# Feed-forward weight sums in half units with two buffers, row norms as columns with a diagonal, and three subtractions on another engine

## The chip, the cores and the metric

The kernel runs on one core of a Trainium2 chip. A core has a matrix engine (TensorE, in the profile PE for its matmuls and PEld for its weight loads), VectorE (DVE), ScalarE (ACT), GpSimd (POOL) and SyncE (SP). Here every data transfer is issued by SP, on one queue. Each engine takes its instructions strictly in order and waits on semaphores for the others. The metric is device microseconds of one execution.

## The reference

One encoder block over 1040 tokens (16 learned ones and 1024) of width 1024, all in float32. A root-mean-square norm feeds one wide input projection. Its parts go to a four-head bidirectional retention in chunks of 128 tokens, and to a bidirectional state-space scan (SSD); both results are projected, gated and merged, and added to the input. A second norm feeds a feed-forward network (FFN), and a last norm ends the block:

```python
y_ret = head_group_norm(y_ret).reshape(b, l, RET_V) * ret_gn_w
y_ret = (jax.nn.silu(g_ret) * y_ret) @ w_ret_out
...
merged = jax.nn.sigmoid(gate_ret) * y_ret + jax.nn.sigmoid(gate_ssd) * y_ssd
h = h + merged @ w_out
f = dw_conv_centred(rms_norm(h, norm_ffn_w) @ w_ffn_up, w_ffn_conv, b_ffn_conv)
fg, fu = _split(f, (D_FF, D_FF))
h = h + (jax.nn.silu(fg) * fu) @ w_ffn_down
...
h = rms_norm(h, final_norm_w)
return h[:, N_META:]
```

where `rms_norm(x, w)` is x / sqrt(mean(x*x) + 1e-6) * w over the 1024 features of a token.

## The kernel before

Features lie on the 128 partitions (eight tiles for 1024) and tokens along the free axis. Float32 products are made of three matmuls on a high and a low half of each operand (`mm3`, lines 143 to 145); a weight tile is loaded as `wraw` (L132), and ACT and DVE split it into `whi` (L135) and `wlo` (L136).

The program runs through these stages, with times of the profiled execution: the first norm and the first projections (0 to 52 us); the retention of heads 0 to 3, each merged step by step with the dense projections of the next head (52 to 520); SSD (520 to 1410); the output projections (1410 to 1810); the second norm and the FFN's first product (1770 to 2210); its second product and the last norm (2210 to the end).

A scheduler places the instructions of each engine: the code only gives lists of steps, and `merge` and `spread` interleave them. Three places matter here.

**The sums.** The FFN's first product multiplies 2 x 2 blocks in a scheme with fewer products, which needs sums of weight blocks. They depend on weights alone, and are made early: `sum_steps` (L488 to 513) gives a load, an add and a store step for each of 22 units, and L566 spreads six units each over the dense steps beside heads 0 to 2, and four beside head 3. A unit loads two tiles of 128 x 1024 (L494 and L495, 512 KB each, single buffers named `ws`), makes four POOL operations of 128 x 512 in place (L501 to 504), and stores both tiles to a scratch tensor in DRAM (L508). The next unit's loads reuse the tiles, so each must wait for a store.

The retention uses POOL too: rotary products `sw` (L338), scaled queries `qd` (L429), and for each chunk two tiny operations on `bs` (L448, L449: variance plus epsilon, to the power of minus one half), which DVE needs to write the normalised `ry` (L451), which PE transposes to `ptr` (L459).

**The norm before the FFN** (`norm2_steps`, L1041 to 1073). Squares are summed over the eight feature tiles into `acc`. `scale` (L1053) multiplies a 128 x 128 matrix of ones with 128 x n sums, so that each partition holds the sums of all n tokens, takes the square root on ACT (L1058) and the reciprocal on DVE (L1059), both 128 x n. `norm` (L1065) multiplies the eight feature tiles of `hb`. Then differences of operands are formed: t1 (L1068), t3 (L1070) and t4 (L1072) on POOL, t2 (L1071) on DVE; each operand is split into a high half (ACT, L1050) and a low half (DVE, L1051). This is done for two rounds of tokens.

**The last norm** (`fin` in `last_down`, L1318 on). For four blocks of 256 tokens: a matmul with ones (L1320), square root (L1321), reciprocal (L1322), and products with eight feature tiles on DVE (L1329) and POOL (L1327), and the stores. The `fin` of a block is placed after the third feature tile of the next block, the last one at the end.

Of the kernel before, what the change touches and what calls it, by code (L numbers as in the profile page):

```python
# [8 lines left out]
F32 = mybir.dt.float32  # L9
# [7 lines left out]
P = 128  # L17
D = 1024
# [77 lines left out]
def hybrid_kernel(ctx, tc, t):  # L96
# [214 lines left out]
    rb = []  # L311
# [175 lines left out]

    def sum_steps(js):  # L488
        steps = []
        tl = {}  # L490

        def load(j):
            a, b = [rb[0].tile([P, 1024], F32, name=f"ws{i}", tag=f"ws{i}", bufs=1) for i in range(2)]
            nc.sync.dma_start(out=a, in_=t["w_up"][j])  # L494
            nc.sync.dma_start(out=b, in_=t["w_up"][NF + j])  # L495
            tl[j] = a, b

        def add(j):
            a, b = tl[j]
            a11, a12, a21, a22 = a[:, :512], a[:, 512:], b[:, :512], b[:, 512:]  # L500
            nc.gpsimd.tensor_tensor(a22, a21, a22, op=ALU.add)  # L501
            nc.gpsimd.tensor_sub(a21, a11, a21)  # L502
            nc.gpsimd.tensor_sub(a11, a22, a11)  # L503
            nc.gpsimd.tensor_sub(a12, a12, a11)

        def store(j):
            for i, x in enumerate(tl.pop(j)):
                nc.sync.dma_start(out=ws_d[j][:, i, :], in_=x)  # L508

        for j in js:  # L510
            for f in (load, add, store):
                steps.append((0.0, lambda f=f, j=j: f(j)))
        return steps

    def spread(a, b):
# [47 lines left out]
    for h in range(HR):  # L563
        steps = ret_steps(h, str_[h])
        dense = ret_dense(h + 1, str_[h + 1]) if h + 1 < HR else z_steps(0)[:-3]
        dense = spread(dense, sum_steps(((0, 6), (6, 12), (12, 18), (18, 22))[h][0] + i for i in range((6, 6, 6, 4)[h])))  # L566
        merge(steps[:-2], dense, left, 3)
        left = steps[-2:]
# [470 lines left out]
    wo = wo_es.enter_context(tc.tile_pool(name="wo", bufs=2, side="right"))  # L1039

    def norm2_steps(r, acc):  # L1041
        t0 = RB[r][0][0]
# [10 lines left out]
        def scale(q):  # L1053
            b0, bn = RB[r][q]
            ps = pm.tile([P, 512], F32, name="psn", tag="psm")
            x = acc[:, b0 - t0:b0 - t0 + bn]
            nc.tensor.matmul(ps[:, :bn], ones, x, start=True, stop=True)
            nc.scalar.activation(x, ps[:, :bn], AF.Sqrt, bias=eps, scale=1.0 / D)  # L1058
            nc.vector.reciprocal(x, x)  # L1059

        def norm(d0, q):
            b0, bn = RB[r][q]
            for d in range(d0, d0 + 4):
# [3 lines left out]
        steps = [lambda: scale(0), lambda: norm(0, 0), lambda: scale(1), lambda: norm(0, 1),  # L1067
                 lambda: put("b11", u[0][0]), lambda: nc.gpsimd.tensor_sub(t1, u[0][1], u[0][0]),  # L1068
                 lambda: norm(4, 0), lambda: put("b21", u[1][0]), lambda: norm(4, 1), lambda: put("t1", t1),
                 lambda: put("b22", u[1][1]), lambda: nc.gpsimd.tensor_sub(t3, u[1][1], u[0][1]),  # L1070
                 lambda: nc.vector.tensor_sub(t2, u[1][1], t1), lambda: put("t2", t2),  # L1071
                 lambda: nc.gpsimd.tensor_sub(t4, u[1][0], t2), lambda: put("t3", t3), lambda: put("t4", t4)]  # L1072
        return steps
# [240 lines left out]
    def last_down():  # L1314
# [3 lines left out]
        def fin(t0, n, acc, last):  # L1318
            ps = pm.tile([P, 512], F32, name="psn", tag="psm")
            nc.tensor.matmul(ps[:, :n], ones, acc[:, :n], start=True, stop=True)  # L1320
            nc.scalar.activation(acc[:, :n], ps[:, :n], AF.Sqrt, bias=eps, scale=1.0 / D)  # L1321
            nc.vector.reciprocal(acc[:, :n], acc[:, :n])  # L1322
            for d in range(KT):
# [137 lines left out]
```

## Time and profile before

| | |
|---|---|
| three timed runs | 2543.72 to 2549.94 us, median 2547.14 us |
| the profiled execution | 2538.35 us |
| its span, first to last instruction | 2536.6 us |
| mean granted TensorE clock | 0.973 |
| PE busy | 2390.3 us, 94% of the span |
| DVE, ACT, POOL busy | 1324.4, 841.2, 786.5 us |
| the stretch that holds the sums | 52.6 us (first load) to 334.3 us (last store) |

The profiled execution was 8.79 us faster than the median of the timed runs, and 1.75 us of its time lie outside the span. A clock of 1.00 in a row is 2.4 GHz; the other level is 1.2 GHz, so that a mean of 0.93 is a mixture of both.

### The profile page before, as it was taken

To read this page: it belongs to the slowest core of one execution; us is meant where nothing else is said; L and a number is where in the kernel's file an instruction comes from. 1 tells how busy PE (TensorE), PEld (TensorE's weight loads), DVE (VectorE), ACT (ScalarE), POOL (GpSimd) and SP (SyncE) were. 2 spreads that over 40 slices of the span, in tenths; PEclk is the share of its full clock that TensorE was granted. 3 is DMA by queue.
4 is the path that set the end of the run, shared out by engine and by line. 5 is a ranking of instruction groups with operands and counts; after the bars stand their busy time and mean duration, and the time that the engine had idled before them with its cause. 6 is when DMAs were issued, how large, how long until landed. Compare 5 with 4: busy or idle time off the path is not lost.

```text
span 2536.6 us, 39605 instructions
## 1 busy us (share of the span) xinstructions
PE 2390.3 (94%) x15836; PEld 2233.6 (88%) x15836; DVE 1324.4 (52%) x1911; ACT 841.2 (33%) x1437; POOL 786.5 (31%) x851
## 2 busy tenths in 40 slices
PE   7888899989999989998999899999899999999997
PEld 7877799988879779888988799999899999998887
DVE  6223234354663563365356434343997777775437
ACT  4211121143353244254323412123454444442204
POOL 2555532113651561373256112222321111110003
PEclk9998999999989999998999999999999999999999
DMA  4666521212571373267146655236444444355111
GB/s 155 215 193 214 197 90 55 61 48 94 158 173 46 129 183 83 70 183 141 52 140 180 173 158 150 88 98 176 132 145 125 118 117 118 116 170 187 67 50 68
DMA packets 162025, 324.43 MB, mean 128 GB/s; under 512 B 20721, under 2 KB 78577, under 8 KB 157745
## 3 DMA queue, kind: packets, MB, share of 16 engines
q1 hardware_dynamic: 161840, 321.90, 42.7%
q8 instruction: 124, 2.03, 0.4%
q14 instruction: 61, 0.49, 0.1%
HBM read 241.57 MB, written 80.27 MB: 127 GB/s over the span
## 4 chain that ended last, share of the span: by engine, by line
PE 65%; DMA 12%; POOL 9%; DVE 7%; issue 3%; ACT 3%; SPq 0%; POOLq 0%; DVEq 0%; ACTq 0%
PE psu L1168 17%; PE psd L143 11%; PE psd L145 11%; PE psd L144 11%; DMA ws<-in_w_up 4%; PE psw L144 3%; PE psw L143 3%; PE psw L145 3%; DMA br<-row 2%; DMA ws<-ws 2%; POOL t L868 1%; POOL ws L503 1%; PE pss L797 1%; POOL ws L502 1%; PE psb L818 1%
## 5 line engine op out<-in xcount | busy, mean ns | idle before, releaser
L143 PE MATMUL psd<-uh,whi 128*128 128x342 f32 (+3 forms) x1376 | 467.5, 340 | 10.6 <-ACT gs L291 6.3
L144 PE MATMUL psd<-ul,whi 128*128 128x342 f32 (+3 forms) x1376 | 447.7, 325 | 0.0
L145 PE MATMUL psd<-uh,wlo 128*128 128x342 f32 (+3 forms) x1376 | 446.6, 325 | 0.0
L135 ACT CAST whi<-wraw 128x1024 fp32r<-128x1024 f32 (+1 forms) x144 | 149.3, 1038 | 515.7 <-PE psd L144 300.1
L136 DVE TENSOR_TENSOR wlo<-wraw,whi 128x1024 fp32r<-128x1024 f32 (+1 forms) x144 | 191.2, 1330 | 214.4 <-ACT whi L135 214.2
L143 PEld LDWEIGHTS psd<-uh,whi 128*128 128x128 f32 (+1 forms) x1376 | 265.0, 193 | 20.7 <-issue 7.9
L144 PEld LDWEIGHTS psd<-ul,whi 128*128 128x128 f32 (+1 forms) x1376 | 264.2, 192 | 7.2 <-issue 6.8
L145 PEld LDWEIGHTS psd<-uh,wlo 128*128 128x128 f32 (+1 forms) x1376 | 263.9, 192 | 0.1
L143 PE MATMUL psd<-whi,uh 128*128 128x256 f32 x768 | 233.5, 304 | 0.4 <-ACT uh L219 0.4
L145 PE MATMUL psd<-whi,ul 128*128 128x256 f32 x768 | 217.1, 283 | 3.2 <-POOL ul L221 2.7
L144 PE MATMUL psd<-wlo,uh 128*128 128x256 f32 x768 | 217.4, 283 | 0.0
L143 PEld LDWEIGHTS psd<-whi,uh 128*128 128x128 f32 x768 | 146.8, 191 | 10.9 <-issue 8.5
L144 PEld LDWEIGHTS psd<-wlo,uh 128*128 128x128 f32 x768 | 147.1, 192 | 5.8 <-issue 5.3
L144 PE MATMUL psw<-ahl,whi 128*128 128x512 f32 (+1 forms) x400 | 148.4, 371 | 1.6 <-DVE ahl L1287 1.6
L145 PEld LDWEIGHTS psd<-whi,ul 128*128 128x128 f32 x768 | 146.4, 191 | 3.9 <-POOL ul L221 3.1
L143 PE MATMUL psw<-ahl,whi 128*128 128x512 f32 (+1 forms) x400 | 147.0, 370 | 0.0
L145 PE MATMUL psw<-ahl,wlo 128*128 128x512 f32 (+1 forms) x400 | 145.8, 366 | 0.0
L143 PE MATMUL psd<-krh,whi 128*128 128x342 f32 x384 | 123.2, 321 | 3.3 <-ACT krh L974 3.3
L144 PE MATMUL psd<-krl,whi 128*128 128x342 f32 x384 | 123.3, 322 | 0.3 <-DVE krl L975 0.3
L145 PE MATMUL psd<-krh,wlo 128*128 128x342 f32 x384 | 123.1, 321 | 0.0
L1227 DVE SCALAR_TENSOR_TENSOR hb<-hb,vec 128x1024 f32<-128x1024 f32 x88 | 111.2, 1280 | 0.4 <-ACT hb L1223 0.2
L1312 DVE TENSOR_TENSOR hb<-psw,hb 128x512 f32<-128x512 f32 x80 | 55.0, 690 | 100.0 <-PE psw L145 99.9
(307 smaller groups left out, 6183.9 us busy)
## 6 DMA issues: line engine op xcount, KB each, us to landing
br<-row SPq DMA_DIRECT2D x32, 1024.0 KB
ws<-in_w_up SPq DMA_DIRECT2D x44, 512.0 KB
ws<-ws SPq DMA_DIRECT2D x44, 512.0 KB
gt<-gate SPq DMA_DIRECT2D x72, 171.0 KB
wraw<-in_w_xbc SPq DMA_DIRECT2D x24, 512.0 KB
wraw<-ws SPq DMA_DIRECT2D x47, 256.0 KB
hb<-ws SPq DMA_DIRECT2D x45, 256.0 KB
act<-hb SPq DMA_DIRECT2D x22, 512.0 KB
```

The costliest lines, as they stand in the source:

```text
L135: nc.scalar.copy(hi[:, :n], raw[:, :n])
L136: nc.vector.tensor_sub(lo[:, :n], raw[:, :n], hi[:, :n].bitcast(F32))
L143: nc.tensor.matmul(ps, ah, bh, start=(i == 0), stop=False)
L144: nc.tensor.matmul(ps, ah, bl, start=False, stop=False)
L145: nc.tensor.matmul(ps, al, bh, start=False, stop=(i == n - 1))
L502: nc.gpsimd.tensor_sub(a21, a11, a21)
L503: nc.gpsimd.tensor_sub(a11, a22, a11)
L797: nc.tensor.matmul(ps, bk(c), st[("xw", d, c)][:n], start=True, stop=True)
L818: nc.tensor.matmul(ps[:n, :], tk("ct", c - 1), st[("pb", c)], start=True, stop=True)
L1168: nc.tensor.matmul(ps[:, :n], a[:, c], b[:, k, :], start=start and k + i == 0, stop=k == 3 and i == 2, skip_group_check=True)
L1227: nc.vector.scalar_tensor_tensor(o[half], f[half][:, 1 + tap:1 + tap + SEQ], V("fconv_w", 3 * fi + tap), o[half], op0=ALU.mult, op1=ALU.add)
L1312: nc.vector.tensor_tensor(hs, ps, hs, op=ALU.add)
```

## The change

The sums are cut into 44 half units. Half unit u takes 256 of the 512 columns of each half row of unit u // 2, so each of its tiles is [128, 2, 256] (256 KB, in pieces of 1 KB) in place of [128, 1024] (512 KB, rows of 4 KB). Each tile name has two buffers. The steps begin with the loads of half units 0 and 1, and after each store comes the load of the half unit two further. Heads 0 to 2 are given twelve half units each and head 3 eight. The POOL operations are 128 x 256.

`row_rms` takes the place of the ones matmul, square root and reciprocal of both norms. With the sums of squares as the stationary operand and one column of ones as the moving one, it gets the token sums as columns (tokens on partitions, two or three columns), takes root and reciprocal of these [w, k] values, scales the identity by them on ACT to a diagonal [w, w] for each column, multiplies ones by the diagonal on PE, which spreads each token's factor over all partitions, and copies the result from PSUM to `acc` on ACT.

The differences t1, t3 and t4 are formed on DVE.

```diff
--- before.py
+++ after.py
@@ -485,32 +485,42 @@
         return steps
 
 
-    def sum_steps(js):
+    def sum_steps(us):
+
+
         steps = []
-        tl = {}
-
-        def load(j):
-            a, b = [rb[0].tile([P, 1024], F32, name=f"ws{i}", tag=f"ws{i}", bufs=1) for i in range(2)]
-            nc.sync.dma_start(out=a, in_=t["w_up"][j])
-            nc.sync.dma_start(out=b, in_=t["w_up"][NF + j])
-            tl[j] = a, b
-
-        def add(j):
-            a, b = tl[j]
-            a11, a12, a21, a22 = a[:, :512], a[:, 512:], b[:, :512], b[:, 512:]
+
+        def part(src, s_):
+            return src.rearrange("p (h s c) -> p s h c", h=2, s=2)[:, s_]
+
+        def load(u):
+            j, s_ = u // 2, u % 2
+            a, b = [rb[0].tile([P, 2, 256], F32, name=f"ws{i}", tag=f"ws{i}", bufs=2) for i in range(2)]
+            nc.sync.dma_start(out=a, in_=part(t["w_up"][j], s_))
+            nc.sync.dma_start(out=b, in_=part(t["w_up"][NF + j], s_))
+            wsum[u] = a, b
+
+        def add(u):
+            a, b = wsum[u]
+            a11, a12, a21, a22 = a[:, 0, :], a[:, 1, :], b[:, 0, :], b[:, 1, :]
             nc.gpsimd.tensor_tensor(a22, a21, a22, op=ALU.add)
             nc.gpsimd.tensor_sub(a21, a11, a21)
             nc.gpsimd.tensor_sub(a11, a22, a11)
             nc.gpsimd.tensor_sub(a12, a12, a11)
 
-        def store(j):
-            for i, x in enumerate(tl.pop(j)):
-                nc.sync.dma_start(out=ws_d[j][:, i, :], in_=x)
-
-        for j in js:
-            for f in (load, add, store):
-                steps.append((0.0, lambda f=f, j=j: f(j)))
+        def store(u):
+            for i, x in enumerate(wsum.pop(u)):
+                nc.sync.dma_start(out=part(ws_d[u // 2][:, i, :], u % 2), in_=x)
+
+        for u in us:
+            if u == 0:
+                steps += [(0.0, lambda: load(0)), (0.0, lambda: load(1))]
+            steps += [(0.0, lambda u=u: add(u)), (0.0, lambda u=u: store(u))]
+            if u + 2 < 2 * NF:
+                steps.append((0.0, lambda u=u: load(u + 2)))
         return steps
+
+    wsum = {}
 
     def spread(a, b):
 
@@ -563,7 +573,7 @@
     for h in range(HR):
         steps = ret_steps(h, str_[h])
         dense = ret_dense(h + 1, str_[h + 1]) if h + 1 < HR else z_steps(0)[:-3]
-        dense = spread(dense, sum_steps(((0, 6), (6, 12), (12, 18), (18, 22))[h][0] + i for i in range((6, 6, 6, 4)[h])))
+        dense = spread(dense, sum_steps(range(12 * h, min(12 * h + 12, 2 * NF))))
         merge(steps[:-2], dense, left, 3)
         left = steps[-2:]
     merge([], z_steps(0)[-3:], left, 2)
@@ -1038,6 +1048,25 @@
     wo_es = ExitStack()
     wo = wo_es.enter_context(tc.tile_pool(name="wo", bufs=2, side="right"))
 
+    def row_rms(x, n):
+
+
+        k = (n + P - 1) // P
+        w = n // k
+        ps = pm.tile([P, 512], F32, name="psn", tag="psm")
+        q = sg.tile([P, 342], F32, name="rms", tag="gt", bufs=2)
+        for i in range(k):
+            nc.tensor.matmul(ps[:w, i:i + 1], x[:, i * w:(i + 1) * w], ones[:, 0:1], start=True, stop=True)
+        r = q[:w, n:n + k]
+        nc.scalar.activation(r, ps[:w, :k], AF.Sqrt, bias=eps[:w], scale=1.0 / D)
+        nc.vector.reciprocal(r, r)
+        ps = pm.tile([P, 512], F32, name="psn", tag="psm")
+        for i in range(k):
+            c = slice(i * w, (i + 1) * w)
+            nc.scalar.activation(q[:w, c], ident[:w, :w], AF.Copy, scale=r[:, i:i + 1])
+            nc.tensor.matmul(ps[:, c], ones[:w], q[:w, c], start=True, stop=True)
+        nc.scalar.copy(x, ps[:, :n])
+
     def norm2_steps(r, acc):
         t0 = RB[r][0][0]
         m = RB[r][0][1] + RB[r][1][1]
@@ -1052,11 +1081,8 @@
 
         def scale(q):
             b0, bn = RB[r][q]
-            ps = pm.tile([P, 512], F32, name="psn", tag="psm")
             x = acc[:, b0 - t0:b0 - t0 + bn]
-            nc.tensor.matmul(ps[:, :bn], ones, x, start=True, stop=True)
-            nc.scalar.activation(x, ps[:, :bn], AF.Sqrt, bias=eps, scale=1.0 / D)
-            nc.vector.reciprocal(x, x)
+            row_rms(x, bn)
 
         def norm(d0, q):
             b0, bn = RB[r][q]
@@ -1065,11 +1091,11 @@
                 nc.vector.scalar_tensor_tensor(hs, hs, V("norm_ffn", d), acc[:, b0 - t0:b0 - t0 + bn], op0=ALU.mult, op1=ALU.mult)
 
         steps = [lambda: scale(0), lambda: norm(0, 0), lambda: scale(1), lambda: norm(0, 1),
-                 lambda: put("b11", u[0][0]), lambda: nc.gpsimd.tensor_sub(t1, u[0][1], u[0][0]),
+                 lambda: put("b11", u[0][0]), lambda: nc.vector.tensor_sub(t1, u[0][1], u[0][0]),
                  lambda: norm(4, 0), lambda: put("b21", u[1][0]), lambda: norm(4, 1), lambda: put("t1", t1),
-                 lambda: put("b22", u[1][1]), lambda: nc.gpsimd.tensor_sub(t3, u[1][1], u[0][1]),
+                 lambda: put("b22", u[1][1]), lambda: nc.vector.tensor_sub(t3, u[1][1], u[0][1]),
                  lambda: nc.vector.tensor_sub(t2, u[1][1], t1), lambda: put("t2", t2),
-                 lambda: nc.gpsimd.tensor_sub(t4, u[1][0], t2), lambda: put("t3", t3), lambda: put("t4", t4)]
+                 lambda: nc.vector.tensor_sub(t4, u[1][0], t2), lambda: put("t3", t3), lambda: put("t4", t4)]
         return steps
 
     pend = None
@@ -1316,10 +1342,7 @@
         ws = [wload(t["w_dn"][4 * (len(PARTS) - 1) + k]) for k in range(nk)]
 
         def fin(t0, n, acc, last):
-            ps = pm.tile([P, 512], F32, name="psn", tag="psm")
-            nc.tensor.matmul(ps[:, :n], ones, acc[:, :n], start=True, stop=True)
-            nc.scalar.activation(acc[:, :n], ps[:, :n], AF.Sqrt, bias=eps, scale=1.0 / D)
-            nc.vector.reciprocal(acc[:, :n], acc[:, :n])
+            row_rms(acc[:, :n], n)
             for d in range(KT):
                 hs = hrow[d][:, t0:t0 + n]
                 if d in ((5, 7) if last else (1, 2, 3, 4, 5, 6, 7)):
```

The order of SP's transfers in the retention of the first heads. `ws` with a number below 300 is the scratch tensor in DRAM, with a higher number a tile; `in_w_up` are the FFN weights. Before:

```order
L495 DMA ws_1727<-in_w_up 128x1024
L494 DMA ws_1726<-in_w_up 128x1024
L508 DMA ws_246<-ws_1727 128x1024
L132 DMA wraw<-in_w_g 128x1024
L508 DMA ws_246<-ws_1726 128x1024
L495 DMA ws_1927<-in_w_up 128x1024
L494 DMA ws_1926<-in_w_up 128x1024
L508 DMA ws_247<-ws_1927 128x1024
L508 DMA ws_247<-ws_1926 128x1024
```

and now:

```order
L500 DMA ws_2455<-in_w_up 128x2x256
L513 DMA ws_250<-ws_2367 128x2x256
L499 DMA ws_2454<-in_w_up 128x2x256
L513 DMA ws_250<-ws_2366 128x2x256
L500 DMA ws_2554<-in_w_up 128x2x256
L513 DMA ws_250<-ws_2455 128x2x256
L499 DMA ws_2553<-in_w_up 128x2x256
L513 DMA ws_250<-ws_2454 128x2x256
```

Before, both tiles of a unit were stored ahead of the next two loads; now a load of the next half unit stands between the stores of this one, and each store is followed by a load into the other buffer.

PE at the first `fin`, whose sums are `acc` in both orders; `psw` are the FFN's second product, `psn` the norm. Before:

```order
L144 MATMUL psw<-ahl,whi 128x256
L145 MATMUL psw<-ahl,wlo 128x256
L1320 MATMUL psn<-acc_23099,cst 128x256
L143 MATMUL psw<-ahl,whi 128x256
L144 MATMUL psw<-ahl,whi 128x256
```

and now:

```order
L145 MATMUL psw<-ahl,wlo 128x256
L1059 MATMUL psn<-cst,acc_23354 128x1 x2
L1067 MATMUL psn<-rms,cst 128x128
L143 MATMUL psw<-ahl,whi 128x256
L1067 MATMUL psn<-rms,cst 128x128
L144 MATMUL psw<-ahl,whi 128x256
L145 MATMUL psw<-ahl,wlo 128x256
```

The one matmul with ones had products of the FFN directly behind it. Now the two column matmuls are followed at once by the first diagonal matmul (L1067), which needs `rms` from ACT; one product stands between it and the second.

DVE at the norm of the first round; L1051 and L1080 write low halves, L1065 and L1091 are the norm's products, L1088 and L1114 sums of the projection. Before:

```order
L1051 TENSOR_TENSOR b11l_15686<-hb,b11h_15685 128x1024
L1088 TENSOR_TENSOR hb<-psd,xr 128x258
L1065 SCALAR_TENSOR_TENSOR hb<-hb,vec,acc 128x256 x2
L1088 TENSOR_TENSOR hb<-psd,xr 128x256
L1065 SCALAR_TENSOR_TENSOR hb<-hb,vec,acc 128x256 x6
L1088 TENSOR_TENSOR hb<-psd,xr 128x258
L1051 TENSOR_TENSOR b21l_15694<-hb,b21h_15693 128x1024
L1051 TENSOR_TENSOR t1l_15690<-hb,t1h_15689 128x1024
L1051 TENSOR_TENSOR b22l_15698<-hb,b22h_15697 128x1024
L1088 TENSOR_TENSOR hb<-psd,xr 128x256
L136 TENSOR_TENSOR wlo<-wraw,whi 128x1024
L1071 TENSOR_TENSOR hb<-hb 128x4x256
```

and now:

```order
L1080 TENSOR_TENSOR b11l_15906<-hb,b11h_15905 128x1024
L1114 TENSOR_TENSOR hb<-psd,xr 128x258
L1094 TENSOR_TENSOR hb<-hb 128x4x256
L1091 SCALAR_TENSOR_TENSOR hb<-hb,vec,acc 128x256 x2
L1114 TENSOR_TENSOR hb<-psd,xr 128x256
L1091 SCALAR_TENSOR_TENSOR hb<-hb,vec,acc 128x256 x3
L1080 TENSOR_TENSOR b21l_15914<-hb,b21h_15913 128x1024
L1091 SCALAR_TENSOR_TENSOR hb<-hb,vec,acc 128x256
L1114 TENSOR_TENSOR hb<-psd,xr 128x258
L1080 TENSOR_TENSOR t1l_15910<-hb,t1h_15909 128x1024
L1080 TENSOR_TENSOR b22l_15918<-hb,b22h_15917 128x1024
L1114 TENSOR_TENSOR hb<-psd,xr 128x256
```

The subtractions L1094 (t1) and L1096 (t3) now stand in DVE's own order; L1068 and L1070 stood in POOL's.

## Rows read from the trace of the kernel before

**Rows 1.** The page, its parts 1 and 4: engine times; shares of the last chain.

```profile
PE 2390.3 (94%) x15836; PEld 2233.6 (88%) x15836; DVE 1324.4 (52%) x1911; ACT 841.2 (33%) x1437; POOL 786.5 (31%) x851
...
PE psu L1168 17%; PE psd L143 11%; PE psd L145 11%; PE psd L144 11%; DMA ws<-in_w_up 4%; PE psw L144 3%; PE psw L143 3%; PE psw L145 3%; DMA br<-row 2%; DMA ws<-ws 2%; POOL t L868 1%; POOL ws L503 1%; PE pss L797 1%; POOL ws L502 1%; PE psb L818 1%
```

**Rows 2.** Windows: from:to, length, busy us (instructions) by engine, granted clock, DMA share, GB/s.

```profile
52.00:335.00 283.00, 241.51 (x1512) 229.06 (x1511) 82.06 (x176) 58.17 (x123) 158.04 (x169) 0.93 0.58 199
...
400.00:520.00 120.00, 119.91 (x854) 114.00 (x853) 46.08 (x124) 23.33 (x48) 23.63 (x56) 1.00 0.20 58
```

**Rows 3.** Windows of the four parts of the stretch that holds the sums.

```profile
52.60:153.40 100.80, 91.06 (x604) 87.28 (x603) 24.18 (x36) 25.88 (x54) 51.11 (x45) 0.97 0.57 202
153.40:235.00 81.60, 61.15 (x344) 57.91 (x343) 26.55 (x64) 12.35 (x22) 48.35 (x59) 0.89 0.61 192
235.00:275.00 40.00, 38.38 (x257) 35.32 (x258) 10.06 (x25) 9.73 (x27) 20.85 (x20) 0.92 0.65 230
275.00:335.00 60.00, 50.32 (x306) 47.95 (x305) 20.88 (x51) 10.04 (x19) 37.15 (x46) 0.91 0.53 185
```

**Rows 4.** Tile ws: ns min/median/max, first and last start; the waits before it.

```profile
L501 POOL TENSOR_TENSOR ws<-ws x22: 1259/1282/1293, 58.9 to 326.8; 128x512 f32<-128x512 f32 x22
...
  POOL ws L501: 93.3, 22
```

**Rows 5.** Chain of waits, 90 to 130 us: start, us, what.

```profile
105.72 3.49 DMA ws<-ws
...
109.23 4.60 DMA ws<-in_w_up
...
113.97 1.30 POOL ws L502
...
118.00 3.74 DMA ws<-ws
```

**Rows 6.** Waits, 50 to 340 us: who for whom, total us, times, longest.

```profile
DVE ry L451 <- POOL bs L449: 94.2, 16, 12.3
...
PE ptr L459 <- DVE ry L451: 23.1, 7, 9.9
```

**Rows 7.** Timeline of POOL, 180 to 192 us: start, us, instruction, idle before it.

```profile
188.07 1.28 POOL L501 TENSOR_TENSOR ws<-ws 128x512 f32<-128x512 f32 x1 [5.70 <-DMA ws<-in_w_up]
189.43 0.22 POOL L448 TENSOR_SCALAR bs<-bs 128x1 f32<-128x1 f32 x1
```

**Rows 8.** Chain of waits, 1410 to 1900 us: transfers of about 256 KB.

```profile
1431.09 4.67 DMA ka<-yr
...
1437.15 2.90 DMA ka<-yr
...
1820.18 3.44 DMA wraw<-ws
```

**Rows 9.** Timeline of DVE, 1776 to 1860 us, in the norm before the FFN.

```profile
1774.48 3.36 DVE L1059 RECIPROCAL acc<-acc 128x256 f32<-128x256 f32 x2 [1.10 <-ACT acc L1058]
...
1790.72 3.33 DVE L1051 TENSOR_TENSOR b21l<-hb,b21h 128x1024 fp32r<-128x1024 f32 x1
1793.98 1.21 DVE L1051 TENSOR_TENSOR t1l<-hb,t1h 128x1024 fp32r<-128x1024 f32 x1
```

**Rows 10.** Timeline of POOL there, and the window 1785 to 1795 us.

```profile
1783.84 2.58 POOL L1068 TENSOR_TENSOR hb<-hb 128x1024 f32<-128x1024 f32 x1
...
1785.00:1795.00 10.00, 5.04 (x40) 4.62 (x38) 10.00 (x11) 4.61 (x5) 5.11 (x3) 0.96 0.18 53
```

**Rows 11.** Timelines of ACT and PE at the final norm.

```profile
2497.74 1.28 ACT L1321 ACT_TABLE_LOAD   x1
...
2525.90 1.22 PE L1320 MATMUL psn<-acc,cst 128*128 128x256 f32 x2 [3.17 <-DVE acc L1345]
```

**Rows 12.** Groups by form: small operations of ACT and DVE, total busy, mean ns.

```profile
L397 ACT ACTIVATE kd<-psk,cst 128x128 f32<-128x128 f32 x60 | 17.9, 366 | 6.2 <-PE psk L392 6.0
...
L465 DVE SCALAR_TENSOR_TENSOR ryt<-ptr,vec,rg 128x2 f32<-128x2 f32 x8 | 1.4, 212 | 4.7 <-PE ptr L459 4.7
```

## The prediction

> **What bounds the kernel now.** I read the page first: PE is busy 2390.3 us of a 2536.6 us span, so about 146 us are to be had there at all, beside what the clock takes [rows 1]. The shares of the last chain then say where other work ends last: next to PE's products stand the loads and stores of `ws`, 4% and 2%, and the additions on them, about 1% a line; together some 200 us of the chain pass through the sums [rows 1]. So the windows of that stretch came next. From 52 to 335 us PE is busy 241.51 of 283 us, at a mean granted clock of 0.93; from 400 to 520 us, retention and dense products without sums, it is busy 119.91 of 120 at 1.00 [rows 2]. The reader is to see that the same kind of work fills PE as soon as the sums are gone.
>
> In its four parts PE lacks 9.7, 20.5, 1.6 and 9.7 us [rows 3]. The tile view gives the pace of the sums: the first operation of a unit starts 22 times from 58.9 to 326.8 us, 267.9 / 21 = 12.76 us a unit, and POOL stood idle before it for 93.3 us until a load landed [rows 4]. The chain shows why: store 3.49, load 4.60, three additions of 1.3 with their gaps, in a ring of 118.00 - 105.72 = 12.28 us [rows 5]. The waits show how PE is drawn in. DVE waited 94.2 us in 16 waits for `bs` from POOL, and PE 23.1 us in 7 for the `ry` that follows [rows 6]; and POOL's timeline shows L501 idle 5.70 us for a load with the tiny L448 directly behind it in the queue [rows 7]. So each late load holds up the retention's next chunk.
>
> **The change, part by part.**
>
> *The sums.* POOL's operations become 88 pairs of half size. One 128 x 512 takes 1.28 us [rows 4]; half of that is 0.64, and I take 0.70 for a start-up share, so POOL works about as long as before. Transfers of 256 KB are not in `ws` yet; near ones took 2.90, 3.44 and 4.67 us [rows 8], while 512 KB took 3.49 to 4.60 [rows 5]. I take 3.6 for load and store, by the middle row and a little for company on the queue. The ring of one buffer is then 3.6 + 3.6 + 3 x 0.70 + 0.3 = 9.6 us, and two buffers run staggered: 4.8 us a half unit, 44 x 4.8 = 211 us in place of 22 x 12.76 = 281. With both transfers at 2.90 it is 4.1 us and 180 in all, with both at 4.67 it is 5.9 and 258. SP's queue, in order, allows the stagger: a store of one half unit and a load of the next alternate, so a waiting store has at most one load behind it that could have gone. The weight loads `wraw` stand in the same queue; each now passes more, but shorter, waits, and I price that at nothing because two raw buffers cover it; if that cover goes, it is rival three.
>
> The Trainium skill, "DMA: Bandwidth & Descriptors" (Bandwidth, its rule, and Anatomy of one DMA), speaks against the cut: it gives every transfer a fixed part of about 2 us, wants large batches, and calls small ones a loss. The rows bear out that halves are far from half as long, 3.44 against 3.49 us; by the rule at its worst, a half at the price of a whole, the ring is (3.49 + 4.60 + 2.4) / 2 = 5.2 us and the sums 231 us, still under 281. The overlap, not the size, is what would have to pay.
>
> What PE makes of it, part by part. Counted in the two orders, the four parts held about 8, 6, 3.5 and 4.5 units, and the same dense work now holds 18, 15, 7 and 4 half units: more sums early, fewer late. At 4.8 us these last 86, 72, 34 and 19 us. In the first part PE's own 91.06 us are then the limit, and I give 94.5 for 100.8. In the second PE's 61.15 would shrink at a full clock (0.89 of the 81.6 us is what it was granted; half-speed time is 2 x 0.11 x 81.6 = 18 us, of which 9 come back), but sums and the chain bn, POOL, DVE, PE of each chunk stay: 78.5 for 81.6. The third is nearly PE's own, 39 for 40. In the fourth few sums are left, and 400 to 520 us is its pattern: 52 for 60, between PE's 50.32 and some waits. Together 264 for 282.4: -18.4 us. The bounds: PE at full clock all along (241.51 less half of 2 x 0.07 x 283, so 222) and a few waits, 235, which is -47; and nothing gained, or a loss of 10 where both transfers cost over 4.67.
>
> *The norm before the FFN.* Two rounds remove four reciprocals of 128 x 256, 3.36 us a pair, from DVE [rows 9], and put four of two or three columns there, at most 0.21 each, the time of a small DVE operation [rows 12]: -5.9. Three subtractions in each round move from POOL (2.58 us) [rows 10] to DVE; a 128 x 1024 one takes 1.21 alone, as the low halves do: +7.3 for six. But beside a POOL operation such a DVE operation took 3.33 in place of 1.21 [rows 9], 2.12 more; for six subtractions that makes some 12.7 us, which go. DVE does about 11 us less (-5.9 + 7.3 - 12.7), and it is the engine that ends this stretch: 10.00 busy of 10, with PE at 5.04 [rows 10]. Part of it stays hidden, since PE has projections of the other round to do, and `acc` still gets its additions on POOL. The new steps on ACT (a root of a few columns, two or three diagonals of 0.37 and a copy of about as much [rows 12]) lie under this. I take -4.5, near the middle of -11 and +1, a loss only if ACT, which also makes the high halves, falls behind.
>
> "GPSIMD Engine Reference" of the Trainium skill (Specifications; Engine selection) says that POOL shares VectorE's memory interfaces and is about half as fast on two inputs; the trace agrees, 2.58 against 1.21 and 3.33 for the disturbed one. By it alone the gain is the whole 11.
>
> *The last norm.* Before, PE went from L1320 into the next products, and root and reciprocal lay beside them. Now the first diagonal stands directly behind the column sums, and PE, in order, waits for root, reciprocal, and a diagonal copy: about 0.3 + 0.2 + 0.37 with four handovers of some 0.1, so 1.3 us; the first time also the table load of 1.28 [rows 11]. Three times inside the blocks: 3 x 1.3 + 1.3 = 5.2; what queues on ACT and DVE ahead of these can add 0.5 each. Products of PE and all that drains them stand behind it. But DVE loses three reciprocals of 1.7 us there, and PE's last product ends 3.17 us before the last sum is ready [rows 11], so some comes back: I take +4, bounds +1 to +7. Behind the last block nothing hides anything: before, a matmul of 1.22 [rows 11], a root of some 0.45 and a reciprocal of 1.68 [rows 9]; now columns 0.6, 0.3, 0.2, two diagonals 0.74, a matmul 0.6 and a copy 0.4 with handovers, 3.0: -0.5 (-1.5 to +0.5).
>
> *Sum.* -18.4 - 4.5 + 4 - 0.5 = -19.4 us. Against the profiled execution, 2538.35, that is 2519; this execution was 8.8 us below the median of the runs shown, so on the median's scale 2547.1 - 19.4 = 2527.7, which I round to 2527.
>
> **The rivals.**
> 1. *PE becomes the only bound.* Freed of late loads, POOL answers the retention at once, and the clock returns to 1.00: for it, the 119.91 of 120; against it, more sums per dense step in the first two parts. Sums -47, the rest -1: 2499.
> 2. *The retention's own chain keeps the time.* DVE, POOL and PE hand over in each chunk whatever the loads do, and the sums were only beside it: for it, PE waits only 23.1 us for `ry` in all; against it, the idle 93.3 us and the chain through `ws`. Sums -5, the rest -1: 2541, or no change.
> 3. *Transfers stretch each other (the slower side).* Twice as many DMAs, in 1 KB pieces, on a queue at 0.58 busy; if they take each other's time, load and store need more than 5.2 us each and the half unit 6.4 = 12.76 / 2. From that point the sums end later than now, weight loads behind them in SP's queue come late, and the stalls of the last norm are on top. At 6.7 us: 44 x 0.3 = +13, with -1: 2559. For it, the spread of 2.90 to 4.67; against it, that the load and store of 512 KB stay below 5 in the chain.
>
> **How the numbers follow.** Forecast 0.60 (its own range 2517 to 2539), rival one 0.14, rival two 0.14, rival three 0.12. A difference of 0.2% (5 us) is about what a measurement of this kernel can tell from none. Faster: 0.60 + 0.14 + half of rival two = 0.81, less 0.03 for the forecast's upper edge: 0.78. Same: 0.07 of rival two and 0.03: 0.10. Slower: 0.12. The range of 8 in 10 cuts the far part of rival one and most of rival three: 2496 to 2549.
>
> **What would show it.** The last store of `ws` at about 52.6 + 215 to 230 us, so 265 to 285, while the first operation of a half unit recurs every 4.8 us and idles about 2 before it; DVE's wait for `bs` under half of 94.2 us; 52 to 320 us with a clock above 0.95. In the norm L1080 at 1.2 throughout and PE less idle at 1785 to 1795. At the last norm PE waits of over 1 us before L1067, three times, the first about 2.5. The forecast is wrong if the sums' pace is above 6 us, or if the pace is right and PE's idle time in that stretch doesn't fall.

## The result, and the profile after

The changed kernel is slower: median 2562.06 us (2557.25 to 2567.85, 5 runs) against 2548.59 us (2543.72 to 2549.94, 5 runs) of before, ratio 1.0058 (1.0037 to 1.0079), which is about +15 us. 2527 with a range of 2496 to 2549 had been forecast. Its profiled execution took 2567.85 us, the slowest of the five, so its span is not to be set against that of before stage by stage without other runs; the retention, though, came out alike in two profiles of these sums. The profile of before errs the other way: its execution, 2538.35 us, was faster than every timed run of that kernel. Its first `ry` comes at 154.3 us, as in e2, e3 and e4 below, which keep the sums of before (152.0 to 154.6), but its last at 502.8, where they have 505.3 to 508.9.

The page of after, parts 1 and 4, answers to [rows 1]:

```profile
PE 2405.6 (94%) x15888; PEld 2248.8 (88%) x15888; DVE 1306.4 (51%) x1917; ACT 850.2 (33%) x1462; POOL 782.4 (30%) x933
...
PE psu L1194 17%; PE psd L143 12%; PE psd L145 12%; PE psd L144 11%; DMA ws<-in_w_up 4%; PE psw L144 3%; PE psw L145 3%; PE psw L143 3%; DMA br<-row 2%; PE pss L807 1%; POOL ws L507 1%; PE psb L828 1%; PE psy L442 1%; DMA ws<-ws 1%; POOL t L878 1%
```

PE is busy 15 us longer than before and idle 160 us, for 146; the shares of the loads stand at 4% as before. The windows of the four parts answer to [rows 3]; they are cut at the same normalised chunks `ry` (the first of head 0, the last of head 0, the first of head 1, the last of head 1 on DVE), except that [rows 3] ended at 335 us, 10 us short of head 1's last:

```profile
52.60:167.00 114.40, 90.98 (x607) 87.22 (x606) 22.39 (x36) 25.80 (x54) 67.07 (x88) 0.91 0.65 203
167.00:258.70 91.70, 60.66 (x346) 56.44 (x344) 24.28 (x64) 12.35 (x22) 60.62 (x94) 0.87 0.66 203
258.70:301.00 42.30, 40.40 (x281) 37.20 (x282) 11.22 (x25) 10.23 (x28) 25.44 (x36) 0.95 0.72 215
301.00:363.00 62.00, 56.86 (x336) 54.47 (x335) 25.74 (x64) 11.47 (x20) 28.45 (x50) 0.94 0.35 111
```

To the first `ry` it is 114.4 us for 100.8, though PE's busy time is the same, 90.98 for 91.06; through head 0 it is 91.7 for 81.6, between the heads 42.3 for 40; only head 1's chunks take less, 62 for 70. The last `ry` of all came at 502.83 us before and at 521.43 now. Set against e2 to e4, the first part holds the whole loss: from the first `ry` to head 1's last it is 195.6 us now and 195.7 to 198.3 there. The tile view of `ws` answers to [rows 4]; its last line is that of before that [rows 4] leaves out:

```profile
L513 SPq DMA_DIRECT2D ws<-ws x88: 359/366/627, 59.3 to 319.1; - x88
L499 SPq DMA_DIRECT2D ws<-in_w_up x44: 540/551/2226, 53.0 to 313.4; - x44
...
L506 POOL TENSOR_TENSOR ws<-ws x44: 721/733/1713, 57.8 to 315.4; 128x256 f32<-128x256 f32 x44
...
  POOL ws L507: 45.0, 31
  POOL ws L506: 42.9, 16
```

```profile
  POOL ws L502: 14.3, 13
```

The first addition of a half unit starts 44 times from 57.8 to 315.4 us, 257.6 / 43 = 5.99 us each. Two make 11.98, against 12.76 for a whole unit. POOL's waits before the sums fell only from 93.3 + 14.3 to 42.9 + 45.0 us, and there are 47 of them for 35 (all for loads but one, 2.3 us for a store). What follows from them answers to [rows 6]:

```profile
DVE ry L451 <- POOL bs L449: 92.4, 14, 11.6
...
PE ptr L459 <- DVE ry L451: 36.3, 10, 13.1
```

DVE still waits 92.4 us for `bs`, and PE's waits for `ry` grew from 23.1 to 36.3 us (in e2 to e4 they are 27.8 to 29.4). Up to 340 us the kernel has now done less of the retention than before; up to 530 us, with all of it done, DVE's waits for `bs` are 115.0 us before and 112.0 now, so they are not where the loss came from. POOL's timeline shows a wait as it is now, with the retention's `sw` (L338) next to the additions:

```profile
127.55 0.92 POOL L338 TENSOR_TENSOR sw<-sw,sin 128x348 f32<-128x348 f32 x1
131.86 0.72 POOL L507 TENSOR_TENSOR ws<-ws,ws 128x256 f32<-128x256 f32 x1 [3.39 <-DMA ws<-in_w_up]
132.66 0.72 POOL L508 TENSOR_TENSOR ws<-ws,ws 128x256 f32<-128x256 f32 x1
133.46 0.72 POOL L509 TENSOR_TENSOR ws<-ws 128x256 f32<-128x256 f32 x1
134.14 0.72 POOL L506 TENSOR_TENSOR ws<-ws 128x256 f32<-128x256 f32 x1
134.82 0.92 POOL L338 TENSOR_TENSOR sw<-sw,sin 128x346 f32<-128x346 f32 x1
```

L507 idles 3.39 us for the load of its second tile, and the next `sw` comes behind four more additions. The first of these `sw` had its input from ACT at 109.2 us and ran at 127.55, behind thirteen additions with 8.0 us of waits for loads among them. The same one before was ready at 108.5 and ran at 117.93, behind four additions of a whole unit. DVE's rotary product `rk` waits for it, and PE for what DVE does next (`rpb`, L406, a copy of the retention state); before, and then now:

```profile
118.88 1.22 DVE L339 TENSOR_TENSOR rk<-rk,sw 128x348 f32<-128x348 f32 x1 [9.81 <-POOL sw L338]
...
PE psk L392 <- DVE rpb L406: 4.1, 1, 4.1
```

```profile
128.50 0.52 DVE L339 TENSOR_TENSOR rk<-rk,sw 128x348 f32<-128x348 f32 x1 [18.75 <-POOL sw L338]
...
136.68 0.48 PE L392 MATMUL psk<-cst,rk 128*128 128x128 f32 x1 [18.59 <-DVE rpb L406]
```

So PE stands still for 18.59 us at once, where it waited 4.1 before. In e1 this wait is 18.1 us, in e2 to e4 3.0 to 5.0; the difference, some 14 us, is what the first part lost (PE is idle for 23.4 us of it, and was for 9.7).

In the norm before the FFN, the reciprocals and the low half of b21 (answering to [rows 9]):

```profile
1805.05 0.17 DVE L1062 RECIPROCAL rms<-rms 128x2 f32<-128x2 f32 x1 [1.65 <-ACT rms L1061]
...
1815.92 1.21 DVE L1080 TENSOR_TENSOR b21l<-hb,b21h 128x1024 fp32r<-128x1024 f32 x1
```

A reciprocal takes 0.17 us for two columns, and b21's low half 1.21 for 3.33. At the last norm, PE's operations of the first two blocks, and the table load, answering to [rows 11]:

```profile
2522.76 0.80 PE L1067 MATMUL psn<-rms,cst 128*128 128x128 f32 x2 [2.30 <-ACT rms L1066]
...
2523.57 0.63 PE L1067 MATMUL psn<-rms,cst 128*128 128x128 f32 x2
```

```profile
2534.83 0.49 PE L1067 MATMUL psn<-rms,cst 128*128 128x128 f32 x2 [1.08 <-ACT rms L1066]
```

```profile
2520.52 1.28 ACT L1061 ACT_TABLE_LOAD   x1
```

PE stands 2.30 and 1.08 us, in the third block 1.61.

### The profile page after: what moved, and what is told of

Same layout as the page of the kernel before. It is cut to its first block, busy times and chain, and to the rows that moved or that the text cites. A ratio compares the mean times of both kernels' runs of the same rounds, so it can differ in the third digit from the quotient of the medians.

```text
span 2566.1 us, 39997 instructions
## 1 busy us (share of the span) xinstructions
PE 2405.6 (94%) x15888; PEld 2248.8 (88%) x15888; DVE 1306.4 (51%) x1917; ACT 850.2 (33%) x1462; POOL 782.4 (30%) x933
## 4 chain that ended last, share of the span: by engine, by line
PE 69%; DMA 11%; POOL 8%; DVE 6%; ACT 3%; issue 3%; SPq 1%; POOLq 0%; DVEq 0%; ACTq 0%
PE psu L1194 17%; PE psd L143 12%; PE psd L145 12%; PE psd L144 11%; DMA ws<-in_w_up 4%; PE psw L144 3%; PE psw L145 3%; PE psw L143 3%; DMA br<-row 2%; PE pss L807 1%; POOL ws L507 1%; PE psb L828 1%; PE psy L442 1%; DMA ws<-ws 1%; POOL t L878 1%
## 5 line engine op out<-in xcount | busy, mean ns | idle before, releaser
L854 DVE TENSOR_TENSOR br<-br,tok 128x2048 f32<-128x2048 f32 (+1 forms) x36 | 83.5, 2319 | 48.9 <-DMA br<-row 48.9
```

The costliest lines, as they stand in the source:

```text
L854: nc.vector.tensor_tensor(r, r, tok[:n, c, 0, g * 16:g * 16 + 16].unsqueeze(2).broadcast_to([n, 16, n]), op=ALU.add)
```

## The experiments

Each is set against runs of the kernel before on the same chip. I first took the change apart, then the sums, whose loss had no place in my prediction.

**E1 to E4: which edit costs what.** Parts of the change put into the kernel before.

```diff
 e1  sum_steps, and the line that spreads it, as changed; nothing else
 e2  row_rms in norm2_steps and in fin, t1 t3 t4 on nc.vector; sums as before
 e3  row_rms in norm2_steps, t1 t3 t4 on nc.vector; the rest as before
 e4  row_rms in fin; the rest as before
```

> Only the half-unit sums; both norms and the subtractions as before. Theory A (the sums lose: 18 half units at 6.0 us in place of 8 units at 12.8 us stand beside the first dense part, so PE starves early and gets back little late): +12 to +18 us, with the first normalised chunk about 13 us later and the last about 18 us later. Rival B (the sums are neutral and the norms cost the time): within 4 us of before.

> Both norms by columns and diagonal, and the subtractions on VectorE; the sums as before. Theory A: -2 to -4 in the norm before the FFN, +5 to +7 at the last norm, so 0 to +5 us. Rival B: +10 to +14 us.

> Columns, diagonal and subtractions in the norm before the FFN alone. Theory A: -2 to -5 us. Rival B, or a diagonal that waits behind the products of PE: +2 to +6 us.

> Columns and diagonal in the last norm alone. Theory A (PE stands at the first diagonal of three blocks, 2.3, 1.1 and 1.6 us, and its products behind): +4 to +7 us. Rival: the three reciprocals of 1.75 us that go from VectorE pay for the stalls: within 1.5 us.

| | median us | before us | ratio | in us |
|---|---|---|---|---|
| e1 | 2564.20 | 2554.21 | 1.0052 (1.0040 to 1.0065) | +13 |
| e2 | 2553.87 | 2554.21 | 1.0009 (0.9996 to 1.0021) | +2 |
| e3 | 2545.74 | 2554.21 | 0.9972 (0.9961 to 0.9983) | -7 |
| e4 | 2559.60 | 2554.21 | 1.0036 (1.0022 to 1.0050) | +9 |

Here and below "in us" is the ratio less one, times the median of before. The sums alone make the loss, within theory A's +12 to +18; e1 also repeats the chunks of after (first `ry` 167.42 us, last 521.89). The two norms nearly cancel: -7 and +9. The norm before the FFN gained a little more than expected, the last norm cost more. E3 holds the columns and the moved subtractions together; they were not tried apart. In e4's profile PE waits 5.9 us in all for the diagonals:

```profile
PE psn L1057 <- ACT rms L1056: 5.9, 4, 2.3
```

From the first of the column matmuls to the end of the span it takes 47.2 us in e4 and 45.4 in e2, and from the matmul with ones 38.9 to 39.4 in before, e1 and e3: 6 to 8 us of the +9. The two differ in the granted clock around the first block, 0.87 in 20 us of e4 and 1.00 in e2 and before.

**E5: how much the sums cost at all.**

```diff
     def sum_steps(js):
+        return []
...
-        s2, s3 = ws_d[j][:, 0, :], ws_d[j][:, 1, :]
+        s2, s3 = a, b
```

> The kernel before without the weight sums: nothing is loaded, added or stored for them beside the retention, and the FFN reads plain weight blocks of the same size in their place, so the FFN's products are of other numbers. It bounds what any form of the sums can give. Theory A (late loads in front of POOL's queue hold the retention up, whatever the cut): -35 to -55 us, with PE near 100% busy from 52 to 520 us as it is after 400. Rival: PE's own chain of retention steps keeps most of the idle time, -5 to -15 us.

2484.76 us against 2554.70, ratio 0.9725 (0.9710 to 0.9740): -70 us, more than either theory said. The FFN then works on plain weight blocks. The same four parts, cut at the same chunks:

```profile
52.60:134.00 81.40, 81.11 (x558) 78.55 (x557) 20.54 (x35) 25.16 (x53) 8.98 (x14) 1.00 0.16 51
134.00:193.00 59.00, 59.00 (x375) 57.13 (x374) 26.20 (x64) 11.84 (x21) 16.55 (x35) 1.00 0.18 52
193.00:228.00 35.00, 34.70 (x251) 32.11 (x250) 10.50 (x25) 10.49 (x29) 4.02 (x7) 1.00 0.12 38
228.00:287.00 59.00, 59.00 (x375) 57.13 (x375) 26.22 (x64) 11.84 (x21) 16.55 (x35) 1.00 0.19 52
```

PE is busy throughout at a clock of 1.00, and the last `ry` comes at 445.22 us. So the sums cost the retention 57.6 us in the profile of before (22 units, 2.6 us each), 60.1 to 63.7 by e2 to e4, and 76.2 us after (44 half units, 1.73 each). Note the first part: 81.4 us, while I had taken PE's busy 91.06 of before for a floor. A part of that difference is work that now stands later (558 matmuls for 604), another is matmuls at the lower clock: over the four parts, the last taken to 345 us, PE was busy 250.9 us before for 1570 matmuls and 233.8 here for 1559.

**E6 and E7: what sets the pace.** Each is e1 with one edit: longer pieces, and stores that don't stand in SP's queue.

```diff
 e6
-            return src.rearrange("p (h s c) -> p s h c", h=2, s=2)[:, s_]
+            return src.rearrange("p (s h c) -> p s h c", h=2, s=2)[:, s_]
 e7
-                nc.sync.dma_start(out=part(ws_d[u // 2][:, i, :], u % 2), in_=x)
+                nc.scalar.dma_start(out=part(ws_d[u // 2][:, i, :], u % 2), in_=x)
```

> The sums in half units alone (norms as before), each half unit taken as 512 columns in one piece of 2 KB for each partition in place of two of 1 KB, so that the sums pair other columns and the FFN's numbers are others. Bytes, number of transfers and order stay. Theory A (SP's order sets the pace: the load of the next half unit stands behind a store that waits for POOL): pace 5.6 to 6.0 us a half unit, time within 5 us of the half units in 1 KB pieces, that is +8 to +15 against before. Rival P (the 1 KB pieces make transfers slow): pace 5.0 or less and most of the loss gone.

> The sums in half units alone, their stores issued by ACT, so no load stands behind a store in SP's queue. Theory A: the pace falls from 6.0 to 4.5 to 5.2 us a half unit; the last half unit is done at about 265 to 285 us instead of 319; the time may still be worse where ACT waits for POOL before a store. Rival P (slow transfers): the pace stays at 5.7 or more.

E6: 2559.38 against 2554.70, 1.0021 (1.0008 to 1.0035), +5 us; pace (308.2 - 57.9) / 43 = 5.82 us. E7: 2590.07, 1.0138 (1.0120 to 1.0155), +35 us; pace 5.80. The first additions of each, e6 and then e7:

```profile
L499 SPq DMA_DIRECT2D ws<-in_w_up x44: 327/430/1456, 52.4 to 307.0; - x44
...
L506 POOL TENSOR_TENSOR ws<-ws x44: 721/734/1002, 57.9 to 308.2; 128x256 f32<-128x256 f32 x44
```

```profile
L506 POOL TENSOR_TENSOR ws<-ws x44: 721/727/1017, 58.2 to 307.8; 128x256 f32<-128x256 f32 x44
...
  ACT sw L334: 53.4, 8
```

Neither theory of the pace holds in both runs. With pieces of 2 KB a half unit still takes 5.82 us, where the theory of slow pieces said 5.0 or less. With the stores out of SP's queue it takes 5.80, where SP's order was to give 4.5 to 5.2; that test is less clean, as the stores now wait in ACT's order. So what sets the pace stays open. The 1 KB pieces cost something, about 8 of e1's 13 us, and 43 times e6's gain in pace (6.01 us in e1) is 8 us as well. In e7 pace and time part: ACT now stands 53.4 us before `sw`, and the kernel is far slower at a slightly better pace, for that reason of its own. So I looked for what each unit does to PE, and not only how fast the sums run.

**E8: the same half units, later.** From e1. A tiny DVE copy from the latest retention state into a tile makes its load wait.

```diff
             new = rb[0].tile([P, 256], F32, name=tag, tag=tag, bufs=8 if d else 2)
...
+            gate["s"] = new[:, 0:1]
             return new
...
+            if gate:
+                for x in (a, b):
+                    nc.vector.tensor_copy(x[:, 0, 0:1], gate["s"])
             nc.sync.dma_start(out=a, in_=part(t["w_up"][j], s_))
```

> The sums in half units alone, and each pair of loads waits for a tiny VectorE copy from the latest retention state, so that the half units are spread over all four heads (5 before the first normalised chunk in place of 19). Theory A (too many sums stand early, and PE starves in front of them at the same pace): -15 to -35 us against before, last store near 500 us. Rival (the cost of a half unit to PE is the same wherever it stands): +5 to +15 us.

2562.40 against 2554.70, 1.0034 (1.0021 to 1.0046), +9 us: the rival was right. Five half units stand before the first `ry` in place of 19, and it comes at 135.23 us, nearly as without sums; but the last comes at 520.23. In the mean a half unit costs 75 / 44 = 1.70 us, about as in the change (1.73), though 39 of the 44 now stand behind the first `ry`. The long wait of the first part is gone, and shorter ones have come later: PE waits 54 us in all up to 530 us here, 62 in e1 and 6 in e5. The waits, from 50 to 520 us:

```profile
DVE ry L454 <- POOL bs L452: 132.9, 33, 8.8
POOL ws L512 <- DMA ws<-in_w_up: 118.3, 25, 7.3
```

The additions follow their loads as closely as before, so POOL waits 118.3 us for loads, and DVE 132.9 us for POOL.

**E9 to E11: transfers, additions, and the wait between them.** From e8: without additions; without transfers; and with additions that wait for a later state.

```diff
 e9   add(u) does nothing
 e10  load(u) only for u < 2, later half units use these tiles; store(u) does nothing; s2, s3 = a, b
 e11, in add(u)
+            if gate:
+                nc.vector.scalar_tensor_tensor(b[:, 0, 0:1], gate["s"], 0.0, b[:, 0, 0:1], op0=ALU.mult, op1=ALU.add)
             nc.gpsimd.tensor_tensor(a22, a21, a22, op=ALU.add)
```

> The paced half units without POOL's additions: the tiles are loaded and stored as they are, so the FFN works on plain weights there. The last normalised chunk stood at 445 us without sums and at 520 with the paced half units. Theory Q (the cost is POOL's queue, where waiting additions stand in front of the retention's own operations): at most 460 us, and the whole 40 to 60 us below the kernel before. Theory D (transfers and SP's order, which delay the weight loads): 490 us or more, and within 25 us of the kernel before.

> The paced half units without their transfers: POOL adds on two pairs of tiles that are loaded once, so it never waits for a load, nothing is stored, and the FFN works on plain weights. Theory Q in its strong form (occupation of POOL alone, 176 operations of 0.73 us): last normalised chunk at 480 us or more, 10 to 30 us below the kernel before. Theory W (only the waits for loads in front of POOL's queue cost, not the additions): at most 460 us, 45 to 65 us below the kernel before.

> The paced half units, and the additions of a half unit wait in addition for a later retention state (a tiny VectorE operation that adds zero times that state to one column), so that a load has more time before POOL reaches the additions; all is computed. Theory W: POOL's waits for loads fall from some 118 us below 50, the last normalised chunk comes at 485 us or earlier, and the whole is 10 to 30 us below the kernel before. Theory Q strong or D: within 10 us of the paced half units, so +0 to +15 against before.

| | median us | ratio to before (2554.90) | in us | last `ry` us |
|---|---|---|---|---|
| e9 | 2490.32 | 0.9758 (0.9732 to 0.9785) | -62 | 447.25 |
| e10 | 2505.52 | 0.9812 (0.9790 to 0.9834) | -48 | 461.35 |
| e11 | 2503.61 | 0.9805 (0.9781 to 0.9829) | -50 | 459.90 |

Against e5's -70, the transfers alone cost 8 us and the additions alone 22; together with the waits, in e8, they cost 79. So about 49 us come only where both meet, as the waits of the additions for their loads would; e11 is the test of that. E9 came out as theory Q said and e10 as theory W said, each within 2 us of its bounds, and e11 gained more than the 10 to 30 us that W gave it. E11 does all the work of e8 and differs by one tiny DVE operation for each half unit, and it is 58 us faster. Its waits and those of the additions only:

```profile
DVE ws L504 <- DMA ws<-ws: 74.1, 44, 5.2
...
POOL ws L514 <- DVE ws L513: 63.9, 31, 4.8
...
DVE ry L454 <- POOL bs L452: 37.8, 30, 3.2
```

```profile
DVE ry L454 <- POOL bs L452: 50.0, 36, 4.3
```

Waits are still there: DVE stands 74.1 us for stores before the gating copies, and POOL 63.9 us before additions. But DVE's wait for `bs` is 37.8 us, at most 3.2, where e8 had 132.9 and up to 8.8, and PE waits 16 us in all for e8's 54. POOL now waits for a state that the retention itself makes, and no longer holds the retention up for a load. POOL's timelines, e8 first, then e11:

```profile
164.44 0.72 POOL L512 TENSOR_TENSOR ws<-ws 128x256 f32<-128x256 f32 x1 [7.31 <-DMA ws<-in_w_up]
165.24 0.72 POOL L513 TENSOR_TENSOR ws<-ws,ws 128x256 f32<-128x256 f32 x1
166.04 0.72 POOL L514 TENSOR_TENSOR ws<-ws,ws 128x256 f32<-128x256 f32 x1
166.84 0.72 POOL L515 TENSOR_TENSOR ws<-ws 128x256 f32<-128x256 f32 x1
167.52 0.45 POOL L432 TENSOR_TENSOR qd<-rq,qdc 128x128 f32<-128x128 f32 x1
167.93 0.91 POOL L338 TENSOR_TENSOR sw<-sw,sin 128x346 f32<-128x346 f32 x1
```

```profile
165.46 0.22 POOL L451 TENSOR_SCALAR bs<-bs 128x1 f32<-128x1 f32 x1 [2.91 <-DVE ws L513]
165.76 0.73 POOL L514 TENSOR_TENSOR ws<-ws 128x256 f32<-128x256 f32 x1
166.46 0.57 POOL L452 TENSOR_TENSOR bs<-bs,mhalf 128x1 f32<-128x1 f32 x1
166.99 0.74 POOL L515 TENSOR_TENSOR ws<-ws,ws 128x256 f32<-128x256 f32 x1
167.81 0.74 POOL L516 TENSOR_TENSOR ws<-ws,ws 128x256 f32<-128x256 f32 x1
168.62 0.73 POOL L517 TENSOR_TENSOR ws<-ws 128x256 f32<-128x256 f32 x1
```

In e8 POOL stands 7.31 us at L512 for a load, and the scaled queries and `sw` come after it. In e11 `bs` (L451, L452) and the four additions run into one another, with no wait for a load among them; the 2.91 us ahead of `bs` are for DVE.

**E12 to E14: a version that beats both, and whether the cut matters.** E12 is e11 with the norm before the FFN as in e3. E13 is e11's two gates on the whole units of before (512 KB, single buffers). E14 is e1 with the gate on the additions alone.

```diff
 e13, in load(j), and in add(j) the same line as e11's on b[:, 0:1]
+            if gate:
+                for x in (a, b):
+                    nc.vector.tensor_copy(x[:, 0:1], gate["s"])
 e14, in add(u) only: e11's line
```

> The paced half units with later additions, and the norm before the FFN by columns and diagonal with the subtractions on VectorE; the last norm as before. All is computed. If the two gains add: -50 and -7, so 2543 to 2552 becomes 2490 to 2500, -53 to -60 us against before. If they overlap: within 4 us of the later additions alone.

> The whole units of before (512 KB, single buffers, 128 x 512 additions), paced by the retention state and with later additions; norms as before. If the place of the additions is all (theory W), the cut and the second buffer matter little: -40 to -52 us. If two buffers are needed for loads to be early enough: -25 us or less, with POOL or VectorE waiting for loads again.

> The half units of the change with the later additions alone: loads go as early as two buffers allow, and only the additions wait for a later retention state; norms as before. Theory W: -45 to -60 us, at least as good as with paced loads. If early loads crowd SP's queue and delay weight loads: -35 us or less.

| | median us | ratio to before (2551.29) | in us |
|---|---|---|---|
| e12 | 2493.38 | 0.9766 (0.9741 to 0.9791) | -60 |
| e13 | 2520.03 | 0.9874 (0.9853 to 0.9895) | -32 |
| e14 | 2516.53 | 0.9865 (0.9842 to 0.9888) | -34 |

E12 beats both kernels; the gains add, within their intervals. E13 lies between what its theories said, and e14 at the edge of the weaker one (-35 or less). Later additions turn the loss of the half units (e1, +13) into -34 without any pacing of loads, so the place of the additions is most of it; the pacing gives another 16 (e11). And with the additions late, paced halves in two buffers (e11) are 18 us better than paced whole units in one; the cut and the second buffer were not told apart. Their waits, e13 and then e14:

```profile
DVE ry L454 <- POOL bs L452: 39.6, 32, 5.2
```

```profile
DVE ry L454 <- POOL bs L452: 54.4, 35, 5.3
```

E14's early loads leave DVE 54.4 us of waits for `bs`, up to 5.3 us, against 37.8 in e11; what in them does it was not tried apart. E13's single waits reach 5.2 us too, behind additions of twice the length; with 39.6 us in all its waits for `bs` do not explain the 18 us, which stay open.

## Why the prediction was wrong

*What bounds the kernel.* Right in its place and in its chain: a late load, an addition that idles at the head of POOL's queue, the retention behind it [rows 5 to 7]. E8 to e11 show that this wait is worth about 50 us with half units; with whole ones, later additions with paced loads won 32 (e13).

*The step that failed* is the one that turned this into a pace: "4.8 us a half unit, 44 x 4.8 = 211 us in place of 22 x 12.76", and with it "what PE makes of it, part by part", where a part took the longer of the sums' time and PE's. Two things are wrong there. The size: a half unit took 5.99 us, just over the far end of 5.9 that I had given to both transfers at 4.67 us. A second buffer lets a ring overlap, but the chain still goes from load to addition to store; the loads of `ws` in the chain of waits there (28 pieces of over 1.5 us after, 22 before) have a median of 3.85 us for a half and 4.47 for a whole, so halving the bytes won little. By the rule of parts itself that pace gives 18 x 5.99 = 108, 15 x 5.99 = 90 and 7 x 5.99 = 42 us for the first three; measured were 114.4, 91.7 and 42.3, forecast 94.5, 78.5 and 39. So in the prediction's own terms most of the miss is this one. And 33 half units stand in the first two parts, where 14 units stood: these lose from 14 x 12.76 / 33 = 5.4 us a half unit on, which the prediction's break-even of 6.4 passed over, and the later parts gave back only 6 us (104.3 for 110).

The other thing is the kind: the pace is no price in itself. In e8 a half unit comes every (516.0 - 57.2) / 43 = 10.67 us, at about the time of e1; in e11 every 9.25 us, and the kernel is 58 us faster. POOL's time in the sums, busy and waiting in order, is what the retention sees: before 4 x 22 x 1.29 + 107.6 = 221 us, after 4 x 44 x 0.735 + 87.9 = 217. The change moved that total by little and put more of it in front: up to the first `ry` it is 84.0 us before (42.8 busy, 41.2 waiting) and 101.5 after (58.3 and 43.2), and there PE's one wait of 18.59 us lies.

I had the fact in hand, "each late load holds up the retention's next chunk", and then let the hold-up vanish with a faster ring. The loads of the change are issued two half units ahead in the code, but in the order the additions stand close behind the loads, and the second buffer only let both stand earlier. I saw 18 half units in the first part in the order and priced their length, at 4.8 us each, not their waits.

*How the sum went.* Part by part I forecast 94.5, 78.5, 39 and 52 us for 100.8, 81.6, 40 and 60. Measured, 114.4, 91.7 and 42.3; the fourth, to head 1's last chunk, 62 for 70. So -18.4 became +18.6 at the last `ry` against the profile of before, and +12.5 to +16.1 against e2 to e4; e1 finds +13 in the time over several runs.

*The norm before the FFN* was right: -4.5 forecast, -7 measured by e3 (0.9961 to 0.9983, -4 to -10), and the trace shows what was named, though not each one's share: the reciprocals went and the stretched operations fell back to 1.2 us. "GPSIMD Engine Reference" of the Trainium skill (Specifications) says the two engines share memory interfaces; the trace agrees with 3.33 against 1.21 us. The whole 11 us that I had worked out from it was not reached.

*The last norm* had its mechanism right and its size too small: +3.5 with the tail, +9 by e4 (+6 to +13). The stalls of 2.30, 1.08 and 1.61 us, 4.99 in all, are the 5.2 I had worked out; that DVE's relief would give some back did not show.

*The rivals.* The slower one named transfers that stretch each other from 6.4 us a half unit on. The time fell on its side, but not by it: the pace was 5.99 us, under its 6.4, the last sums were done earlier than before, and the kernel was slower all the same. The Trainium skill's rule against cutting transfers was nearer than my estimate: "DMA: Bandwidth & Descriptors" (Anatomy of one DMA) has a fixed part, which it gives for transfers issued by GpSimd, while these are issued by SP. The trace agrees in that halves were not half as long, 3.85 against 4.47 us. But e13 against e11 shows halves, with their second buffer, worth 18 us once no addition waits, so the rule alone would have misled as well.

## What to carry to other kernels

On an engine that works in order, ask of every instruction that waits for a transfer what stands behind it; the cost here was that wait, not the rate of the side work, and a second buffer did not pay while the consumer stood close behind the load. Count, too, how much of the side work an edit puts in front of the main work: 19 half units stood before the first `ry` where 8 units had. Where a scheduler puts the consumer close behind the load, tie the consumer to something the main work produces later: one tiny operation for each half unit was worth 58 us here. And a busy time taken at a clock below 1.00 is no floor, so take the stage without the side work as the bound before pricing an edit of it.

## What the runs showed of the hardware

A load of a tile in two pieces of 1 KB for each partition held SP 0.55 us (both tiles in after, medians), the same bytes in one piece of 2 KB 0.43 and 0.33 (e6). For the stores the two took 0.37 and 0.33 us. DMA issues that wait for another engine stall the engine that issues them: stores from ACT held it up before `sw` for 53.4 us (e7).
